# New numbers in the hold-back table of a merged decoder-layer kernel

## The chip, the cores and the metric

One core of one Trainium2 chip runs the whole program. The metric is device time in microseconds of one execution; a kernel's time is the median of its runs. "PE" is the tensor engine, "DVE" the vector engine, "ACT" the scalar engine, "POOL" GpSimd, "SP" the engine that issues most DMAs.

## The reference

One layer of a hybrid decoder runs over a prompt (512 tokens and 16 meta tokens) and over 8 samples of 8 tokens each, with the same float32 weights. Cut to what matters:

```
xn = rmsnorm(x, ln_mix_pre)
q, k, v, gdn_qkv, z, b, a, gate_a, gate_b = split(xn @ w_in)
o_a = diff_attention(q, k, v)                # samples: 16 cached pages of 128 keys each
o_b = gated_delta(silu(conv(gdn_qkv)), b, a) # 4 heads, a recurrence over chunks
o_b = rmsnorm(o_b) * silu(z)
mix = sigmoid(gate_a) * (rmsnorm(o_a) @ w_branch_a) + sigmoid(gate_b) * (o_b @ w_branch_b)
x = x + rmsnorm(mix @ w_out)
up, gate = split(rmsnorm(x) @ w_ffn_in)
x = x + rmsnorm((gelu(conv(gate)) * up) @ w_down)
```

Outputs are the two activations, the new keys and values, and the new states of the delta rule and of both convolutions.

## The kernel before, in words

Each float32 weight tile is split into a high and a low part (`split`, L314 on ACT and L315 on DVE), and a product is three matmuls: high by high, high by low, low by high (`project`, `dense_steps`). A weight tile is 128 columns of a matrix; the tokens are taken in two halves (256 and 336, or 256 and 322 columns). Such dense products write to PSUM tiles `ps_d`. Weight tiles arrive through SP in three `wraw` buffers. Pages of the key and value cache arrive through SP too, 128 of each, in five `page` buffers of two pages.

The program has three stretches. First the input is normalised and transposed and the queries are made. Then comes a merged stretch. Last come the sum of the branches, the output projection and the feed-forward part.

The merged stretch is where this change lies. `Body.merge` takes several generators, called streams. A stream emits a few instructions, then yields a number. `mm` and `transpose` add the price of each PE instruction to a counter `work`: 0.42 ns for each column of a matmul of the split parts, 1.68 ns for one of plain float32, 0.11 us for a transpose. A stream that has yielded `d` may go on when the counter has grown by `d`. So the number is a distance in PE work: while a link of one stream runs through DVE or ACT, PE is given that much work of the other streams. Among the streams that may go on, the one that has spent the smallest part of its share goes first. Where none may go on, a counter `idle` grows in steps of 0.1 and counts as work.

`merge` decides the order in which the instructions are written down. The framework under it then takes that order as priority: it may move an instruction that is ready ahead of one that isn't, when it lays down each engine's list. The lists themselves are fixed before the program runs, and each engine works through its own in order, with semaphores for what comes from the others.

The streams:

- `da_main`: `da_keys` makes keys and values of the four prompt heads (hold 21 after the second half of each), `prompt_attention` works through rows of 128 queries (24 after the scores, 25 after the transposes of the weights, 23 after the head norm), then the meta tokens (22).
- `gdn`: for each head h, `gdn_chain` and, beside it, `gdn_project` of head h + 1 (0 after the last convolution). The chain makes decays (1), transposes and norms (2 to 5), the first inverse by DVE alone (`gdn_base`, 12), the rest of the inverse by products (`gdn_solve`, 13 to 17), and then a recurrence: the tail of samples and meta tokens (6, 7, 8), and four chunks, each of `gS` times `kk` to `grhs` (9), `grhs` to `gv` (10), and `gv` to the next `gS` (11). The head ends with the product `z` (`gdn_gate`) and the transposes of `on`. `gdn_solve_tail` has the holds 18 to 20 in a loop over levels.
- `rest`: `sample_attention` for four pairs of samples, first scores against pages of keys (26), the softmax over 2112 columns (27), then products with pages of values (28), the scaling (29), and after each second pair a head norm (30). Then the 16 gates (`gate`), and `branch_a`, the product of `w_branch_a`, which waits for `self.spare`, set when the last head's solve begins.

In the prediction a step of the recurrence is named as in r, v, S with head and chunk: v00 is the product that gives `gv` of head 0, chunk 0, and S20 the one that gives the next state of head 2.

Of the kernel before, what the change touches and what calls it, by code (L numbers as in the profile page):

```python
# [52 lines left out]
def _lay_out_constants():  # L53
# [76 lines left out]


DELAY = (
    10.08, 5.4, 0.6, 0.6, 6.0, 1.3, 0.9, 0.85, 1.32, 1.0, 1.68, 0.17, 26.0, 0.67, 2.93, 0.77,
    0.09, 0.85, 0.38, 2.28, 0.05, 1.54, 0.74, 1.56, 6.12, 0.84, 1.4, 11.52, 1.4, 1.68, 10.28,
)
KEYS = 2
CUT_S = 832
# [2071 lines left out]
```

## Time and profile before

| | |
|---|---|
| runs of the kernel before | 1165.96, 1167.31, 1167.40 us |
| their median | 1167.31 us |
| span of the profiled execution, first to last instruction | 1165.2 us |
| median of the runs less that span | 2.1 us |
| mean granted clock of the tensor engine | 0.995 |
| PE busy from 60 to 640 us | 563.46 of 580 us |
| DMA share from 60 to 640 us | 0.53 |

The page gives the span of the profiled execution; its time as a run is not listed apart. A page lists the busy time of each engine, the busy share in slices of the span, the DMA queues, the chain of work that ended last, and groups of instructions. In the rows of busy time by stretch each engine's busy microseconds stand in the order PE, PEld (weight loads), DVE, ACT, POOL, then the granted clock, the share of the DMA engines and GB/s. A row of the list of waits reads: who waited, for whom, microseconds in total, how often, the longest. A row of a timeline reads: start, duration, engine, line, operation, tiles, count, and in brackets the idle time before it. Matmuls overlap, so the duration of one is longer than its distance to the next.

### The profile page before, as it was taken

The numbers are of one execution on the slowest core, as the hardware profiler recorded it, in microseconds if no ns is written. First come the engines' busy times: TensorE is split into PE (matmuls) and PEld (weight loads), VectorE is DVE, ScalarE is ACT, GpSimd is POOL, SyncE is SP. The second block draws the span as 40 slices with busy tenths as digits, with TensorE's granted clock in tenths as the row PEclk, the third lists the DMA queues.
The fourth block names the chain that finished last, engine by engine and source line by source line (L and its number), as shares of the span: only waits on it lengthen the run. The fifth ranks groups of instructions, "written<-read, shape, count | busy, mean of one in ns | idle before, by whom it ended". The sixth has DMA issues, their size and how long they took to land.

```text
span 1165.2 us, 23602 instructions
## 1 busy us (share of the span) xinstructions
PE 1122.8 (96%) x8683; PEld 1006.0 (86%) x8683; DVE 717.9 (62%) x1875; ACT 540.1 (46%) x1308; POOL 221.2 (19%) x342
## 2 busy tenths in 40 slices
PE   6999999989999999999999999999999999999997
PEld 5987788777777687689999987899999999999996
DVE  5446667578377368357234675399888988842323
ACT  5234545455355355353333345365556555832331
POOL 2122131030020020010000003234444454200000
PEclk9999999999999999999999999999999999999999
DMA  7374333936847766722222364133333332432322
GB/s 205 80 247 139 108 99 109 300 116 206 298 142 240 259 215 201 245 76 73 73 68 71 99 181 159 68 110 101 92 92 103 90 102 73 143 91 78 100 74 82
DMA packets 184347, 157.56 MB, mean 135 GB/s; under 512 B 12570, under 2 KB 146273, under 8 KB 184231
## 3 DMA queue, kind: packets, MB, share of 16 engines
q1 hardware_dynamic: 179713, 147.53, 41.3%
q0 software_dynamic: 3264, 5.16, 1.5%
q10 hardware_dynamic: 1254, 3.35, 1.0%
q8 instruction: 69, 1.13, 0.4%
q14 instruction: 47, 0.39, 0.1%
HBM read 146.12 MB, written 9.88 MB: 134 GB/s over the span
## 4 chain that ended last, share of the span: by engine, by line
PE 75%; issue 11%; DVE 7%; ACT 2%; POOL 2%; DMA 2%; SPq 0%; DVEq 0%; POOLq 0%; ACTq 0%
PE ps_d L272 29%; PE ps_t L272 18%; PE ps_g L272 15%; PE ps_t L420 7%; PE ps_s L272 6%; PE ps_m L272 1%; DMA page<-in_cache_v 1%; DVE cy L650 1%; DMA page<-in_cache_k 1%; DVE row L970 0%; POOL hss L384 0%; DVE row L971 0%; DVE xc L972 0%; DVE wlo L315 0%; ACT KT L1399 0%
## 5 line engine op out<-in xcount | busy, mean ns | idle before, releaser
L272 PE MATMUL ps_d<-xhi,whi 128*128 128x256 f32 (+2 forms) x704 | 218.4, 311 | 0.0
L272 PE MATMUL ps_d<-xhi,wlo 128*128 128x256 f32 (+2 forms) x704 | 213.9, 304 | 0.8 <-DVE wlo L315 0.8
L315 DVE TENSOR_TENSOR wlo<-wraw,whi 128x512 fp32r<-128x512 f32 x196 | 137.3, 717 | 125.1 <-ACT whi L314 123.9
L272 PE MATMUL ps_d<-xlo,whi 128*128 128x256 f32 (+2 forms) x704 | 213.5, 303 | 0.3 <-DVE xlo L315 0.2
L314 ACT CAST whi<-wraw 128x512 fp32r<-128x512 f32 (+1 forms) x198 | 116.6, 612 | 176.1 <-PE ps_d L272 99.7
L272 PEld LDWEIGHTS ps_d<-xhi,whi 128*128 128x128 f32 x704 | 133.9, 190 | 8.1 <-issue 4.6
L272 PEld LDWEIGHTS ps_d<-xlo,whi 128*128 128x128 f32 x704 | 134.0, 190 | 4.5 <-issue 3.3
L272 PEld LDWEIGHTS ps_d<-xhi,wlo 128*128 128x128 f32 x704 | 134.0, 190 | 1.7 <-DVE wlo L315 1.0
L1399 ACT COPY KT<-ps_t 128x512 f32<-128x512 f32 x106 | 57.5, 596 | 37.6 <-PE ps_t L420 36.2
L420 PE MATMUL ps_t<-consts,page 128*128 128x128 f32 x512 | 68.4, 278 | 1.3 <-DMA page<-in_cache_k 1.0
L420 PEld LDWEIGHTS ps_t<-consts,page 128*128 128x128 f32 x512 | 55.8, 140 | 14.7 <-issue 8.4
L272 PE MATMUL ps_t<-fhit,hw 128*128 128x290 f32 x228 | 68.0, 298 | 0.0
L272 PE MATMUL ps_t<-flot,hw 128*128 128x290 f32 x228 | 67.7, 297 | 0.0
L272 PE MATMUL ps_t<-fhit,lw 128*128 128x290 f32 x228 | 67.6, 297 | 0.0
L314 ACT CAST hw<-sw 128x512 fp32r<-128x512 f32 x76 | 47.2, 623 | 41.2 <-PE ps_g L272 19.9
L315 DVE TENSOR_TENSOR lw<-sw,hw 128x512 fp32r<-128x512 f32 x76 | 59.6, 784 | 6.7 <-ACT hw L314 6.6
L272 PEld LDWEIGHTS ps_t<-flot,hw 128*128 128x128 f32 x228 | 43.3, 190 | 0.0
L272 PEld LDWEIGHTS ps_t<-fhit,lw 128*128 128x128 f32 x228 | 43.1, 189 | 0.0
L272 PEld LDWEIGHTS ps_t<-fhit,hw 128*128 128x128 f32 x228 | 43.0, 189 | 0.0
L272 PE MATMUL ps_s<-KT,qb 128*32 128x256 f32 x512 | 37.1, 385 | 0.4
L1887 DVE SCALAR_TENSOR_TENSOR fy<-fpre,fw,fy 128x592 f32<-128x592 f32 x44 | 36.5, 830 | 1.0 <-ACT fy L1885 0.2
L908 POOL DMA_DIRECT2D out_new_gdn_sample<-st x4 | 3.8, 941 | 170.5 <-ACT gv L892 86.0
(688 smaller groups left out, 3025.8 us busy)
## 6 DMA issues: line engine op xcount, KB each, us to landing
page<-in_cache_k SPq DMA_DIRECT2D x128, 256.0 KB, 4.5
page<-in_cache_v SPq DMA_DIRECT2D x128, 256.0 KB, 4.2
wraw<-in_w_in SPq DMA_DIRECT2D x88, 256.0 KB, 2.9
wraw<-in_w_ffn_in SPq DMA_DIRECT2D x50, 256.0 KB, 3.1
wraw<-in_w_down SPq DMA_DIRECT2D x40, 256.0 KB, 3.2
raw<-in_w_ffn_in SPq DMA_DIRECT2D x38, 256.0 KB, 2.8
wraw<-in_w_out SPq DMA_DIRECT2D x16, 256.0 KB, 2.9
x<-in_x_prompt SPq DMA_DIRECT2D x4, 512.0 KB, 8.9
```

Of the source, the lines that this page charges most:

```text
L272: return self.nc.tensor.matmul(out, lhsT, rhs, **kw).ins
L314: self.nc.scalar.copy(hi, raw)
L315: (eng or self.nc.vector).tensor_tensor(out=lo, in0=raw, in1=hi.bitcast(F32), op=ALU.subtract)
L420: self.nc.tensor.transpose(out, in_, self.ident[:k, :k])
L650: nc.vector.scalar_tensor_tensor(out=y, in0=pre[:, j : j + n], scalar=self.cw[:, ch, 24 + j : 25 + j], in1=y, op0=ALU.mult, op1=ALU.add)
L908: nc.gpsimd.dma_start(o["new_gdn_sample"][0, :, h].rearrange("b k v -> k b v"), state)
L1399: copy(kt[:, :, 128 * j : 128 * j + 128], tp)
L1887: nc.vector.scalar_tensor_tensor(out=y, in0=pre[:, j : j + 592], scalar=fw[:, m, 16 + j : 17 + j], in1=y, op0=ALU.mult, op1=ALU.add)
```

## The change

It replaces numbers in the tuple `DELAY`. The tuple has 31 entries, counted from 0; its first row holds 0 to 15, its second 16 to 30. Nothing else changes: neither the instructions nor their number, nor sizes and buffers.

```
 DELAY = (
-    10.08, 5.4, 0.6, 0.6, 6.0, 1.3, 0.9, 0.85, 1.32, 1.0, 1.68, 0.17, 26.0, 0.67, 2.93, 0.77,
-    0.09, 0.85, 0.38, 2.28, 0.05, 1.54, 0.74, 1.56, 6.12, 0.84, 1.4, 11.52, 1.4, 1.68, 10.28,
+    13.61, 3.59, 0.94, 0.6, 6.0, 1.52, 1.66, 1.43, 1.32, 1.05, 0.93, 0.17, 26.0, 0.69, 0.9, 0.77,
+    0.09, 0.85, 0.38, 2.28, 0.14, 0.6, 0.74, 2.36, 6.91, 0.77, 1.4, 5.18, 1.38, 1.46, 12.26,
 )
```

The largest steps, by ratio, are those of 10 (1.68 to 0.93), 14 (2.93 to 0.9), 21 (1.54 to 0.6) and 27 (11.52 to 5.18), which get smaller, and of 2, 6, 7 and 23, which grow by about a half or more. Entry 20 is changed too (0.05 to 0.14), but its loop is empty here.

## The prediction

> **What bounds the kernel now.** I read the page first, then the busy time by stretch, then who TensorE (PE) waited for in the stretch that the table governs, and last the timelines around the longest of those waits.
>
> ```profile
> span 1165.2 us, 23602 instructions
> PE 1122.8 (96%) x8683; PEld 1006.0 (86%) x8683; DVE 717.9 (62%) x1875; ACT 540.1 (46%) x1308; POOL 221.2 (19%) x342
> ...
> 60.00:500.00 440.00, 424.44 (x3672) 333.94 (x3671) 274.60 (x969) 213.63 (x586) 71.82 (x137) 1.00 0.61 195
> 500.00:640.00 140.00, 139.02 (x1046) 134.70 (x1045) 65.52 (x182) 51.02 (x137) 6.39 (x7) 1.00 0.26 69
> 640.00:700.00 60.00, 58.38 (x392) 54.33 (x393) 40.62 (x74) 23.09 (x42) 0.00 (x0) 1.00 0.47 138
> ```
>
> PE is busy for 96% of the span, no other engine for more than 62%: the kernel is as long as PE's work plus PE's pauses. The table removes and adds no instruction; it only changes the order in which merged streams are written down. So the change is worth what it does to PE's pauses between about 60 us and 660 us. From 60 to 500 PE is idle for 440 − 424.44 = 15.6 us, from 500 to 640 for 1.0 us. Nearly all that can be won lies in the first stretch. These are its waits, and under them the one just behind:
>
> ```profile
> PE ps_t L420 <- DVE kn L792: 3.1, 2, 1.6
> PE ps_t L420 <- DVE on L1344: 2.5, 3, 1.1
> PE ps_g L272 <- DVE grhs L882: 1.8, 4, 0.4
> PE ps_s L272 <- DMA page<-in_cache_v: 1.2, 2, 0.8
> PE ps_t L420 <- DMA page<-in_cache_k: 1.0, 1, 1.0
> PE ps_g L272 <- ACT gv L892: 0.7, 2, 0.4
> PE ps_t L420 <- DVE oS L1344: 0.3, 2, 0.2
> ...
> PE ps_d L272 <- DVE gt L1512: 1.4, 1, 1.4
> ```
>
> The largest, kn (3.1 us), stands behind DELAY[4], which keeps its 6.0. The next, on L1344, stands behind DELAY[23], which changes; grhs and gv stand behind DELAY[9] and [10].
>
> **How much the written order rules.** It does not rule alone: the framework moves instructions that are ready ahead of others. In the plan the split of `oa` comes after all sixteen gates; in the trace it begins at 500.1 us, while the blocks of `z` and the gates' matmuls are still to run. A new number is therefore a preference, not a wait, and most of the new numbers will move nothing that PE feels.
>
> ```profile
> L314 ACT CAST pre<-oa x1: 675/675/675, 500.1 to 500.1; 128x578 fp32r<-128x578 f32 x1
> 635.74 0.28 PE L272 MATMUL ps_d<-kt,whi 128*128 128x256 f32 x1
> 637.14 0.31 PE L272 MATMUL ps_d<-kt,whi 128*128 128x322 f32 x1
> ```
>
> The last two rows give the exchange rate. Twelve 256-column matmuls lie between them: 1.40 us, which the code prices at 12 × 256 × 0.42 ns = 1.29. One unit of the table is about 1.085 us of PE. I also worked the merge rule through with the code's prices for both tables, to see which steps change places.
>
> **Part by part.** *DELAY[23], 1.56 to 2.36 (head norm of the prompt).*
>
> ```profile
> 107.95 0.39 PE L272 MATMUL ps_t<-vt,aT 128*128 128x128 f32 x2
> 110.41 0.17 DVE L383 TENSOR_SCALAR hss<-hss 128x4 f32<-128x4 f32 x1
> 112.27 1.14 DVE L1344 SCALAR_TENSOR_TENSOR on<-on,hss,sub 128x128 f32<-128x128 f32 x4 [1.69 <-POOL hss L384]
> 112.77 0.30 PE L420 MATMUL ps_t<-consts,on 128*128 128x128 f32 x1 [1.09 <-DVE on L1344]
> ```
>
> From the last product (ends 108.34) to the end of the norm (113.41) are 5.1 us, or 4.7 units. Both numbers are under it, the new one by less. It puts 0.8 units, 0.87 us, of other work ahead of the transposes. Of three waits (2.5 us, the longest 1.1) two of about 1.1 shrink to 0.2 and the third goes: −2.0 us. Bounds: 0, if that work isn't ready either, and −2.5.
>
> *DELAY[27], 11.52 to 5.18 (softmax of the sample pairs).*
>
> ```profile
> 460.96 0.43 PE L272 MATMUL ps_s<-kTs,qb 128*32 128x64 f32 x16
> 462.23 2.06 ACT L1479 ACTIVATE S<-S,nm 128x2112 f32<-128x2112 f32 x1 [3.45 <-DVE nm L1477]
> 465.21 0.38 PE L420 MATMUL ps_t<-consts,S 128*64 128x128 f32 x2
> ```
>
> The scores end at 461.39, the exponentials at 464.29: 2.9 us, 2.7 units. 5.18 still covers it, 11.52 was four times too long, yet the transposes of S already start 0.9 us after it, since the framework had moved them up. So the gain is about 0; what changes is that the values' pages stand earlier against the solve of the delta rule. Bounds: −1 us (those 0.9) and, if the pages come too late for it, the page waits of 2.2 us once more.
>
> *DELAY[9], [10] (1.0 to 1.05, 1.68 to 0.93; links of the recurrence).*
>
> ```profile
> 490.08 1.07 PE L272 MATMUL ps_s<-page,pT 128*32 128x256 f32 x16
> 491.08 0.49 PE L272 MATMUL ps_g<-grhs,xy 128*128 128x128 f32 x2
> 491.93 0.49 PE L272 MATMUL ps_g<-gv,kn 128*128 128x128 f32 x2 [0.35 <-ACT gv L892]
> 492.86 0.49 PE L272 MATMUL ps_g<-gS,kk 128*128 128x128 f32 x2
> 493.79 0.49 PE L272 MATMUL ps_g<-grhs,xy 128*128 128x128 f32 x2 [0.45 <-DVE grhs L882]
> ...
> 469.42 17.44 SPq L1378 DMA_DIRECT2D page<-in_cache_v  x22
> 486.96 1.49 SPq L310 DMA_DIRECT2D wraw<-in_w_in  x3
> ```
>
> A link without cover costs 0.35 and 0.45 us. In this head (h = 2) the next weights are issued only at 486.96, behind 22 pages that hold the SP queue for 17.4 us, so there is no dense work to put between. A smaller or larger delay brings none. By the worked order the last pages of pair 3 end one step deeper in the recurrence (at S20 instead of v20), so one link more lies beside pages: −0.8 us. Bounds: −2.5 (1.8 + 0.7, all of it) and +5.0: heads 0 and 1 have no such waits, and each would have 2.5 if its cover went.
>
> In head 3, DELAY[10] is felt as an order:
>
> ```profile
> 614.90 0.38 PE L272 MATMUL ps_g<-gS,kk 128*128 128x128 f32 x2
> 616.90 0.39 PE L272 MATMUL ps_g<-grhs,xy 128*128 128x128 f32 x2
> 619.97 0.38 PE L272 MATMUL ps_g<-gv,kn 128*128 128x128 f32 x2
> ...
> 633.40 0.67 PE L420 MATMUL ps_t<-consts,on 128*128 128x128 f32 x5
> 637.29 2.77 DVE L315 TENSOR_TENSOR blo<-ob,bhi 128x578 fp32r<-128x578 f32 x4
> ```
>
> Between grhs and gv lie 3.07 us, two groups of twelve gate matmuls, where the copy needs far less than one (the wait without any cover was 0.35). With 0.93 one group stands there in each link. PE loses nothing, the chain gets shorter. Head 3 then ends beside gates 12 and 13, not beside the first branch (the rows at 633.40 and 637.29). The 2.77 us of `blo` on DVE no longer stand ahead of the branch's evacuation (gt L1512), for which PE waited 1.4 us: −1.4 us. Bounds: −1.4 and +1.4, if another DVE block takes that place.
>
> *DELAY[21], 1.54 to 0.6 (keys and values of the prompt).*
>
> ```profile
> 104.53 0.31 PE L272 MATMUL ps_d<-xhi,wlo 128*128 128x336 f32 x1
> 105.25 0.43 ACT L1170 COPY kvt<-ps_d 128x336 f32<-128x336 f32 x1
> ```
>
> From the last product (ends 104.84) to the end of the copy (105.68) 0.84 us pass; 0.6 units are 0.65 us. That is short by 0.2, eight times (four heads, keys and values): between 0 and +1.5 us. I take +0.7, the middle, as some of the eight have ready work beside them.
>
> *DELAY[14], 2.93 to 0.9 (the solve's inner products).*
>
> ```profile
> 465.43 0.98 PE L272 MATMUL ps_g<-dd,lm 128*128 128x32 f32 x8
> 466.44 0.27 ACT L1031 COPY dd<-ps_g 128x128 f32<-128x128 f32 x1 [0.66 <-PE ps_g L272]
> 467.29 0.98 PE L272 MATMUL ps_g<-dd,xy 128*128 128x32 f32 x8
> ```
>
> The product ends at 466.41, its copy at 466.71; 0.9 units are 0.98 us: covered, 0. If that cover goes, a wait like that for gv (0.35) eight times: +2.8.
>
> The other thirteen: [20] is never reached, since the tail's list of levels is empty. [30], 10.28 to 12.26, can win no more than the 0.3 us of oS. [6] and [7] (0.9 to 1.66, 0.85 to 1.43) have no wait in the list, nor have [0], [1], [2], [5], [13], [24], [25], [28], [29]; moving them costs at most another kn, 1.6 us, and I take 0.
>
> **Sum.** −2.0 − 0.8 − 1.4 + 0.7 = −3.5 us, from 1165.2 to 1161.7. The median of the runs, 1167.31, is 2.1 us over the profiled span, so 1163.8.
>
> **Weighing a rule of the skill.** The rows give PE 15.6 us of idle time from 60 to 500. They also show PEld busy for 333.94 of 440 us (76%) there and 134.70 of 140 (96%) from 500 to 640. The Trainium skill, Perfetto Trace Analysis, Identifying the Most-Contended Engine, says that matmul occupancy is a poor measure of PE's headroom and that the load-weights share should be used. By that rule the room is an estimated 440 − 333.94 / 0.96 = 92 us, not 15.6, though this stretch holds other kinds of matmul than the next. The trace does not decide here what part of it order can reach.
>
> **The rivals.**
> *Slower: the recurrence loses its cover.* With [27] halved, pages are used up sooner beside the solve, and the links of heads 0 and 1 come after them, as in head 2 now. For it: the worked order ends pair 1's pages ahead of the first link (S0) where they went on to v00 before. Against: in those heads dense work of the next head was at hand. It decides where the first wraw issue after the pages is later than the first gS product. Price: the gains of [23] and the end stay out, 2 × 2.5 = +5.0 us: 1172.3.
> *No change: the framework undoes it.* It moved the split of `oa` up, it can restore most of the old order: 1167.3.
> *More than the idle time.* Small pauses under the limit of the waits' list close up too, as PEld's 76% suggests. A tenth of the difference between 424.44 and 333.94 would be 9 us: 1158.3.
>
> **How the numbers follow.** About 0.2% (2.3 us) is what a measurement of this kernel can tell. Forecast 0.40, more 0.07, no change 0.23, slower 0.30. The first two are faster: 0.47. The range: below, the sum's good ends, −2.5 − 1 − 2.5 − 1.4 − 0.3 = −7.7, and a part of the third rival: 1159.0; above, the slower rival: 1172.5.
>
> **What would show it.** Right: on L1344 under 0.7 us in PE's waits; gt L1512 gone at the branch's start; head 3's last transposes of `on` before the last gates. Wrong: grhs and gv over 4 us, with waits in heads 0 or 1; a wait for kvt or dd in PE's list; page waits over 3 us. If none of these rows moves by 1 us, the second rival holds.

## The result, and the profile after

The median of four runs is 1153.18 us (1151.31 to 1154.48), against 1166.91 us (1165.96 to 1167.40) for the kernel before on the same chip: a ratio of 0.9883, 95% interval [0.9869, 0.9897]. That is 13.7 us faster. The direction was forecast; the size was not: 3.5 us were forecast, and the range ended at 1159.0.

The page of the kernel after begins so; busy time falls by 7.5 us on PE and hardly anywhere else:

```profile
span 1152.0 us, 23616 instructions
PE 1115.3 (97%) x8683; PEld 1004.1 (87%) x8683; DVE 717.3 (62%) x1875; ACT 539.0 (47%) x1308; POOL 220.5 (19%) x342
```

Busy time by stretch, after (PE, PEld, DVE, ACT, POOL, granted clock, DMA share, GB/s):

```profile
60.00:160.00 100.00, 98.39 (x784) 81.54 (x783) 62.60 (x233) 46.58 (x124) 23.89 (x52) 1.00 0.53 166
60.00:500.00 440.00, 429.85 (x3765) 343.85 (x3764) 282.07 (x995) 219.52 (x606) 70.41 (x138) 1.00 0.62 196
500.00:640.00 140.00, 139.77 (x1060) 136.77 (x1059) 64.15 (x173) 46.52 (x121) 5.60 (x5) 1.00 0.29 74
60.00:640.00 580.00, 569.62 (x4823) 480.62 (x4822) 346.22 (x1167) 266.03 (x725) 76.01 (x143) 1.00 0.54 167
```

The same view of before, for the two stretches that the prediction does not show:

```profile
60.00:160.00 100.00, 98.39 (x743) 78.88 (x744) 60.95 (x226) 46.31 (x122) 24.42 (x48) 0.98 0.51 161
60.00:640.00 580.00, 563.46 (x4716) 468.64 (x4714) 340.13 (x1151) 264.65 (x721) 78.21 (x143) 1.00 0.53 165
```

By 640 us PE has issued 107 matmuls more than before. At 580 / 4716 = 0.123 us each that is an estimated 13.2 us, the whole difference of the spans (1165.2 − 1152.0). So all of the gain lies in the merged stretch. But PE's idle time there fell only from 16.5 to 10.4 us. More than half of the gain is not in PE's idle time. The first 100 us show it plainest: PE is busy 98.39 us in both kernels, yet after does 41 matmuls more in them, and PEld is 2.7 us busier. Part of this is the granted clock: the profiled execution of before has 3.41 us at half rate here, at 81 us (mean 0.98), and after has none. Those cost up to 1.7 us, or some 13 of the 41 matmuls at 98.39 / 743 = 0.13 us each. The rest I read as pauses of fractions of a microsecond between matmuls, which a busy row covers.

Where the gain falls I took from a sum of my own, an estimate: each PE instruction priced by its columns, both traces compared at the same time. After is ahead by 4.1 us at 160 us, by 4.6 at 240, 8.5 at 260, 8.5 at 480, 12.1 at 500 and 13.7 at 640. So there are four places: the prompt's first heads (4.1, with up to 1.7 of it the clock), head 0's `kn` (3.9), head 2's links (3.6), and the end of head 3 (1.6).

The waits of PE, after, from 55 to 640 us:

```profile
PE ps_t L420 <- DVE on L913: 2.0, 2, 1.3
PE ps_t L420 <- DVE on L1344: 1.8, 3, 0.9
PE ps_s L272 <- DMA page<-in_cache_v: 1.6, 2, 1.2
PE ps_t L420 <- DVE kn L792: 1.2, 1, 1.2
```

The waits for grhs, gv and gt L1512, 3.9 us before, are gone from the list. Those for kn fell from 3.1 to 1.2, those for on L1344 only from 2.5 to 1.8. Those for on L913 rose from 0.9 to 2.0.

Head 2's recurrence, after: SP's queue, then PE.

```profile
441.80 35.45 SPq L1378 DMA_DIRECT2D page<-in_cache_v  x32
477.36 1.83 SPq L310 DMA_DIRECT2D wraw<-in_w_in  x3
...
473.21 0.39 PE L272 MATMUL ps_g<-gS,kk 128*128 128x128 f32 x2
473.35 0.39 PE L272 MATMUL ps_d<-xhi,wlo 128*128 128x322 f32 x1
...
474.43 0.49 PE L272 MATMUL ps_g<-grhs,xy 128*128 128x128 f32 x2
474.68 0.39 PE L272 MATMUL ps_d<-xhi,wlo 128*128 128x322 f32 x1
...
475.27 0.49 PE L272 MATMUL ps_g<-gv,kn 128*128 128x128 f32 x2
475.69 1.07 PE L272 MATMUL ps_s<-page,pT 128*32 128x256 f32 x16
```

Between every two products of a chunk now stands a group of the next head's dense product (ps_d) or of pages. Before, the last links stood bare. The pages end at 485.2 instead of beyond 494, and the weights are issued at 477.36 instead of 486.96. But the recurrence itself begins earlier by as much: its first product of gS and kk stands at 473.21 instead of 483.96. Against it the weights come no earlier, and the last pages stand at the same step in both kernels, behind the third chunk's grhs product. What changed is the dense work kept for the links: from the first gS by kk product to the last, PE starts 24 dense matmuls after and none before. They begin with weights issued ahead of the pages, as SP issues none from 420 to 477.36.

Head 3, after:

```profile
569.59 0.38 PE L272 MATMUL ps_g<-grhs,xy 128*128 128x128 f32 x2
571.23 0.39 PE L272 MATMUL ps_g<-gv,kn 128*128 128x128 f32 x2
...
600.11 0.67 PE L420 MATMUL ps_t<-consts,on 128*128 128x128 f32 x5
603.40 2.77 DVE L315 TENSOR_TENSOR blo<-ob,bhi 128x578 fp32r<-128x578 f32 x4
```

From grhs to gv are 1.64 us here, and 1.4 to 2.0 in the other three links (before, 2.8 to 3.1 in the first three and 1.2 in the last). `blo` starts 16 us ahead of the branch (first product 619.85) instead of in it. From the first product of gS and kk to these transposes are 32.2 us (567.95 to 600.11), against 35.7 before (597.75 to 633.40). So the shorter links bring 3.5 us of the 33.3 by which the head ends earlier; it also starts 29.8 us earlier.

### The profile page after: what moved, and what is told of

It is laid out like the page before. It is cut to its first block, busy times and chain, and to the rows that moved or that the text cites. A ratio compares the mean times of both kernels' runs of the same rounds, so it can differ in the third digit from the quotient of the medians.

```text
span 1152.0 us, 23616 instructions
## 1 busy us (share of the span) xinstructions
PE 1115.3 (97%) x8683; PEld 1004.1 (87%) x8683; DVE 717.3 (62%) x1875; ACT 539.0 (47%) x1308; POOL 220.5 (19%) x342
## 4 chain that ended last, share of the span: by engine, by line
PE 73%; issue 13%; DVE 6%; ACT 3%; POOL 3%; DMA 1%; SPq 0%; DVEq 0%; POOLq 0%; ACTq 0%
PE ps_d L272 26%; PE ps_t L272 18%; PE ps_g L272 15%; PE ps_s L272 7%; PE ps_t L420 7%; ACT KT L1399 1%; PE ps_m L272 1%; DVE cy L650 1%; DMA lk<-in_da_lambda_k 1%; POOL grr L384 1%; POOL gf L384 0%; DVE wlo L315 0%; DMA page<-in_cache_v 0%; POOL hss L384 0%; DVE row L970 0%
## 5 line engine op out<-in xcount | busy, mean ns | idle before, releaser
L272 PE MATMUL ps_s<-page,pT 128*32 128x256 f32 x512 | 35.3, 385 | 1.8 <-DMA page<-in_cache_v 1.6
L272 PE MATMUL ps_s<-KT,qb 128*32 128x256 f32 x512 | 35.7, 385 | 0.6
```

The lines of the kernel that those rows point to most:

```text
L272: return self.nc.tensor.matmul(out, lhsT, rhs, **kw).ins
```

## The experiments

All times are medians of runs beside the kernel before on the same chip, of which the median was 1166.7 to 1167.5 in each group.

**Four parts alone, in the old table.** Two theories: each number acts on its own wait, and the parts add up; or some numbers are right only together.

*Prompt.*

```
-[21] 1.54  [23] 1.56  [24] 6.12  [25] 0.84
+[21] 0.6   [23] 2.36  [24] 6.91  [25] 0.77
```

> The old table with only the four numbers of the prompt's attention new (21, 23, 24, 25). Theory A, every number pays at its own place and the places add up: the changed kernel is about 4 us ahead by 160 us of the span, so about 4 us faster than before (1163). Theory B, the order is one whole, in which any change moves everything behind it, and parts do not add up: anywhere from 4 us faster to 4 us slower, and unrelated to those 4 us.

Measured 1159.72 us, ratio 0.9939 [0.9921, 0.9958]: 7.7 us faster.

*Samples.*

```
-[27] 11.52  [28] 1.4   [29] 1.68  [30] 10.28
+[27] 5.18   [28] 1.38  [29] 1.46  [30] 12.26
```

> The old table with only the four numbers of the sample attention new (27 to 30), above all 27 halved. Theory A: pages stand earlier against the solve, so the recurrence of head 2 has weights at hand; the unfilled links there cost 2.5 us of waits, so 2 to 4 us faster (1164). Theory B: anywhere within 4 us on either side.

Measured 1178.94, 1.0097 [1.0076, 1.0118]: 11.5 us slower, with 8.7 us of waits for pages of values.

*Solve and recurrence.*

```
-[6] 0.9   [7] 0.85  [9] 1.0   [10] 1.68  [13] 0.67  [14] 2.93
+[6] 1.66  [7] 1.43  [9] 1.05  [10] 0.93  [13] 0.69  [14] 0.9
```

> The old table with only the six numbers of the solve and the recurrence new (6, 7, 9, 10, 13, 14). Theory A: head 3's chain ends earlier, so the wait of 1.4 us at the branch goes, and no more than 1 us elsewhere: 1 to 3 us faster (1165). Theory B: anywhere within 4 us on either side.

Measured 1173.40, 1.0054 [1.0038, 1.0069]: 5.9 us slower.

*Set-up of the heads.*

```
-[0] 10.08  [1] 5.4   [2] 0.6   [5] 1.3
+[0] 13.61  [1] 3.59  [2] 0.94  [5] 1.52
```

> The old table with only the numbers of the chain's set-up new (0, 1, 2, 5; 20 is never reached). Theory A: the waits for kn, 3.1 us before and 1.2 in the changed kernel, shrink: 2 to 4 us faster (1164). Theory B: anywhere within 4 us on either side.

Measured 1171.80, 1.0032 [1.0017, 1.0046]: 4.3 us slower.

(Entry 20, whose loop is empty, was changed along with these four, and put back with them below.)

None of the four came where the first theory had put it, and three moved by clearly more than the 4 us that the second allowed. The four sum to +14.0 us where the whole change gives −13.7. So they do not add: some of these numbers belong together.

**Which belong together.** *Samples with solve, old table.*

```
-[6] 0.9   [7] 0.85  [9] 1.0   [10] 1.68  [13] 0.67  [14] 2.93
+[6] 1.66  [7] 1.43  [9] 1.05  [10] 0.93  [13] 0.69  [14] 0.9
-[27] 11.52  [28] 1.4   [29] 1.68  [30] 10.28
+[27] 5.18   [28] 1.38  [29] 1.46  [30] 12.26
```

> The old table with the sample numbers (27 to 30) and the solve numbers (6, 7, 9, 10, 13, 14) new together; alone they cost 11 and 6 us. Theory P, the two are a pair: the halved softmax hold brings the value pages forward, the short holds of the solve let its products alternate with them; either alone leaves one side bare. Then both together are faster than before by 3 to 7 us (1161 to 1164), and the run of page products without a product between them, and its wait for pages of 8.7 us, is gone. Theory S, the parts add up: 17 us slower (1184). Theory B, no structure: anywhere within 10 us of before.

Measured 1160.11, 0.9941 [0.9924, 0.9957]: −6.6 us, where the two alone cost 11.5 and 5.9. They are a pair. The waits for pages of values, 8.7 us with the samples alone, are 2.3. With the prompt's −7.7 that makes −14.3, close to the change's −13.7.

*The new table with the prompt's four put back.*

```
-[21] 0.6   [23] 2.36  [24] 6.91  [25] 0.77
+[21] 1.54  [23] 1.56  [24] 6.12  [25] 0.84
```

> The new table with the four prompt numbers (21, 23, 24, 25) put back. Theory P, with the prompt numbers worth 7 us on their own stretch: 5 to 8 us slower than the changed kernel (1159 to 1161). Theory S: 1174, as the three other groups alone cost 11, 6 and 4. Theory B: anywhere between.

Measured 1158.10, 0.9921 [0.9906, 0.9936]: some 4.4 us over the change (0.9883). In the new table the prompt's four are worth less than the 7.7 us that they win in the old.

*The new table with the set-up put back.*

```
-[0] 13.61  [1] 3.59  [2] 0.94  [5] 1.52
+[0] 10.08  [1] 5.4   [2] 0.6   [5] 1.3
```

> The new table with the set-up numbers (0, 1, 2, 5, 20) put back. Theory P: they do little on their own, 0 to 3 us slower than the changed kernel (1153 to 1156). Theory S: 4 us faster than it (1149), since alone they cost 4. Theory B: as much as 8 us slower.

Measured 1154.61, 0.9889 [0.9873, 0.9904], as the change itself (0.9883): inside the new table the set-up's numbers neither win nor cost anything that can be measured.

*The new table with the long softmax hold.*

```
-[27] 5.18
+[27] 11.52
```

> The new table with entry 27 alone put back to 11.52. Theory P: the pair is broken, the solve runs ahead of the pages and the links lie bare, 3 to 7 us slower than the changed kernel (1156 to 1160), with waits for grhs and gv back in PE's list. Theory of the prediction (a softmax hold that covers is as good as another): within 1 us of the changed kernel.

Measured 1172.12, 1.0037 [1.0017, 1.0057]: set against the change (1.0037 to 0.9883) some 18 us lost by one number. Both theories missed this: one expected 3 to 7 us with waits for grhs and gv, the other at most 1. No wait for grhs or gv is in the list; those for kn are 4.0 us and for pages of values 4.0. SP's queue and PE show the order that came:

```profile
462.19 1.49 SPq L310 DMA_DIRECT2D wraw<-in_w_in  x3
481.69 16.09 SPq L1378 DMA_DIRECT2D page<-in_cache_v  x22
...
475.35 2.05 PE L272 MATMUL ps_g<-st,zk 128*128 128x128 f32 x16
480.04 0.62 PE L272 MATMUL ps_s<-page,pT 128*32 128x256 f32 x2
```

The whole solve, up to `zk` at 475, has gone by before the first page is used at 480. SP issues nothing for 18 us between, and then the pages run beside the recurrence and into the next head's set-up.

**One number at a time, old table.**

```
-[27] 11.52
+[27] 5.18
```

> The old table with entry 27 alone new (5.18). Theory P: the four sample numbers alone cost 11 us because of this one, so 8 to 12 us slower than before (1175 to 1179), with PE's waits for value pages above 5 us and a stretch at half clock behind them. If 28 to 30 carry it: within 2 us of before.

Measured 1181.72, 1.0140 [1.0116, 1.0163]: 14.8 us slower, somewhat more than expected, with 8.2 us of waits for pages of values. So the harm of the four sample numbers comes from [27].

```
-[14] 2.93  [27] 11.52
+[14] 0.9   [27] 5.18
```

> The old table with entries 27 and 14 new: the halved softmax hold and the hold between the solve's products, 2.93 to 0.9. Theory P in its narrow form, these two are the pair: 4 to 8 us faster than before (1159 to 1163), the solve's products between the page products. In its wide form, all ten numbers of sample and solve are needed: no better than before.

Measured 1165.61, 0.9990 [0.9974, 1.0006]. [14] takes back all of what [27] costs. But the −6.6 us of the pair are not there yet: grhs and gv still have 1.6 us of waits in it, so the solve's other numbers ([6], [7], [9], [10], [13]) or the samples' other three are needed for the links. PE starts no dense matmul between the links of head 2 in this run, and 24 in the run of samples with solve. With the six numbers of the solve alone these waits are gone too, though that run is slower.

```
-[21] 1.54
+[21] 0.6
```

> The old table with entry 21 alone new (1.54 to 0.6). By the prediction it costs 0 to 1.5 us. If the 7 us of the four prompt numbers are its own, since transposes and copies of keys and values come earlier and the rows of the prompt start earlier: 5 to 7 us faster (1160 to 1162).

Measured 1167.22, 1.0001 [0.9989, 1.0013]: nothing that can be measured. No wait for kvt came.

```
-[23] 1.56
+[23] 2.36
```

> The old table with entry 23 alone new (1.56 to 2.36). By the prediction 2.0 us faster, from the waits on L1344 (2.5 us before). If the order behind it matters more than that wait: anywhere within 5 us, while the wait itself changes by less than 1 us.

Measured 1165.17, 0.9980 [0.9965, 0.9995]: 1.7 us, and the wait for on L1344 falls from 2.5 to 1.4. Waits that the number doesn't stand ahead of fall as well: kn from 3.1 to 1.8, grhs from 1.8 to 0.9.

**Is it the softmax's cover, or the place of two streams against each other?** By the merge rule worked through (the working isn't shown here), before and after have pages of values and products of the solve by turns, and with [27] alone nearly all pages come first. The traces agree at pair 3: with [27] alone, 64 products of pages, 16 pages, stand from 477.78 us on without a product of the solve between them; before and after have at most 18 without one. Only the difference of two holds decides: [27] ahead of the pages, and [12] ahead of the solve, which the change doesn't touch. So the harm must go if [12] is moved along, and come without [27] if [12] is moved the other way.

```
-[12] 26.0  [27] 11.52
+[12] 20.0  [27] 5.18
```

> Table of before with entry 27 at 5.18 and entry 12 at 20.0 instead of 26.0. Theory of phase (27 counts only by where the values' pages fall against the solve, and the hold ahead of the solve, 12, moves the solve as far as 27 moved the pages; the worked order of pages against solve of pairs 1 to 3 is then again that of before): the 14.8 us that 27 alone cost go, 1163 to 1170 us, and page waits under 3 us where 27 alone had 8.2. Rival (5.18 is too little for the softmax itself, or too much else moves up with it): 12 doesn't mend it, 1178 to 1184 us. Second rival (20.0 no longer covers the first inverse, whatever the phase): slower than before by over 5 us, with a new wait ahead of the solve.

Measured 1165.87, 0.9990 [0.9974, 1.0006]: the 14.8 us are gone, and the waits for pages of values are 2.5 us instead of 8.2.

```
-[12] 26.0
+[12] 32.34
```

> Table of before with only entry 12 at 32.34 instead of 26.0, the solve held back by as much as the new 27 brings the pages forward. Theory of phase: the same harm without any change to the softmax's hold, 1175 to 1184 us, and page waits over 5 us at the pages of pairs 1 to 3. Rival (the harm of 27 alone is that of the softmax's cover): nothing of it, 1163 to 1170 us, as a longer hold only gives more cover to the first inverse.

Measured 1184.21, 1.0145 [1.0121, 1.0169]: 17.5 us slower, with the softmax's hold untouched. Page waits were 4.8 us, just under the 5 expected. Both runs fall to the theory of place, and the cover of the softmax is out as a cause. PE at pair 3's pages, first with [12] at 20.0 beside the short softmax hold:

```profile
470.40 1.07 PE L272 MATMUL ps_s<-page,pT 128*32 128x256 f32 x16
471.89 1.00 PE L272 MATMUL ps_g<-dd,xy 128*128 128x64 f32 x8
473.48 1.07 PE L272 MATMUL ps_s<-page,pT 128*32 128x256 f32 x16
474.48 0.68 PE L272 MATMUL ps_g<-xy,dbig_low 64*64 64x64 f32 x8
```

and with [12] at 32.34 alone, PE and then the stretch's busy time:

```profile
476.86 1.85 PE L272 MATMUL ps_g<-dd,lm 128*128 128x64 f32 x8 [1.08 <-DVE dd L1010]
478.63 3.64 PE L272 MATMUL ps_s<-page,pT 128*32 128x256 f32 x32
483.24 1.93 PE L272 MATMUL ps_s<-page,pT 128*32 128x256 f32 x16 [0.97 <-DMA page<-in_cache_v]
487.73 1.93 PE L272 MATMUL ps_s<-page,pT 128*32 128x256 f32 x16 [2.56 <-DMA page<-in_cache_v]
...
480.00:500.00 20.00, 14.70 (x100) 8.79 (x93) 3.46 (x12) 3.73 (x10) 0.58 (x1) 0.50 0.41 125
```

SP's queue in the latter:

```profile
465.34 17.49 SPq L1378 DMA_DIRECT2D page<-in_cache_v  x22
```

By turns, each group of pages lies in a link of the solve. In one run, PE uses pages faster than SP's queue brings them (eight pages, 32 products, in 3.64 us even at a clock of 0.50, against 22 in 17.49 us, 0.8 each), waits, and then does the solve bare. The granted clock of that stretch is 0.50; more on that below.

*The counterpart in the new table.*

```
-[14] 0.9
+[14] 2.93
```

> The new table with entry 14 back at 2.93. Theory of phase (14 and 27 are a pair): the worked order puts nearly all of the pages of a pair ahead of the rest of the solve, as with 27 alone, so 1163 to 1172 us, 10 to 19 us over the changed kernel, with page waits over 4 us. Rival (14 mended only what the old numbers of the solve made necessary): within 3 us of the changed kernel, 1150 to 1156 us.

Measured 1173.45, 1.0047 [1.0029, 1.0065], with 9.5 us of page waits: set against the change (1.0047 to 0.9883) some 19 us slower, just past the range expected by the theory of place and far from its rival. So [14] is worth 16 to 19 us beside the new [27], and it was put at nothing in the prediction. How much of this goes through the granted clock is estimated at the end.

**What the prompt's gain is made of.**

```
-[24] 6.12  [25] 0.84
+[24] 6.91  [25] 0.77
```

> Table of before with entries 24 (6.12 to 6.91) and 25 (0.84 to 0.77) new. If these two carry the prompt's gain (7.7 us for the four, of which 21 and 23 alone gave -0.3 and 1.7): 1160 to 1163 us. If the gain lies in the four together: 1165 to 1168 us. If they cost, over 1169 us.

Measured 1166.83, 0.9992 [0.9978, 1.0006]. The runs reach from 1160.59 to 1168.17, and follow the mean clock: 0.996 in the fastest, 0.990 in the four of 1166.9 to 1168.2. In the profiled execution (clock 0.996, span 1158.8) the order's gain is there, while PE's idle time changes by only 0.57 us:

```profile
60.00:160.00 100.00, 98.96 (x775) 81.22 (x774) 62.01 (x230) 46.93 (x124) 24.75 (x52) 0.98 0.52 164
```

32 matmuls more than before in the first 100 us, at the same mean clock of 0.98 and with a half-rate stretch near 81 us too.

```
-[23] 1.56  [24] 6.12  [25] 0.84
+[23] 2.36  [24] 6.91  [25] 0.77
```

> Table of before with 23, 24 and 25 new, 21 left at 1.54. If the prompt's gain is 23 together with 24 and 25: 1158 to 1161 us, as with all four (1159.7). If the parts add: 1.7 + 0.2 off, 1164 to 1166 us, and 21, which alone gave nothing, is needed for the rest.

Measured 1160.43, 0.9947 [0.9929, 0.9965]: −6.6 us. This is the prompt's gain within the intervals (0.9939 with [21]); [21] has no measurable part in it.

**A version built on this.** Longer covers for what still waits, with [12] cut so that the solve stays where it was:

```
-[4] 6.0  [12] 26.0  [23] 2.36
+[4] 7.0  [12] 25.0  [23] 4.0
```

> The new table with 23 at 4.0 (the norm took 4.6 to 6.0 us), 4 at 7.0 (wait for kn 1.2 us left) and 12 at 25.0, so that the solve starts where it did and the worked order of pages against solve stays that of the changed kernel. Theory of phase: no harm, and up to 0.9 of the wait for on and the 1.2 for kn go: 1151 to 1153.5 us. Rival (any longer hold costs as much elsewhere): 1154 to 1158 us.

Measured 1157.90, 0.9923 [0.9908, 0.9938]: 4.7 us slower than the change. The rival holds. The waits aimed at did go, on L1344 from 1.8 to 0.7 and kn from the list, but others came:

```profile
PE ps_s L272 <- DMA page<-in_cache_v: 2.3, 2, 1.5
PE ps_t L420 <- DVE gss L759: 1.7, 1, 1.7
PE ps_d L272 <- ACT tail L631: 1.2, 1, 1.2
PE ps_t L272 <- DVE pT L1453: 1.0, 1, 1.0
```

No kernel run here beats the changed one.

## Why the prediction was wrong, point by point

**What held.** PE's pauses in the merged stretch were the thing to count. [21] was put at +0.7; alone it is +0.3 with an interval of −1.3 to +1.5, and no wait for kvt came. Two terms were met in the number and only in part in the mechanism, so some of that is luck. [23] was put at −2.0 and measured −1.7 alone, but its own wait gave 1.1 of the 2.0, and waits elsewhere went. At the end of head 3 the 1.4 us went as forecast, with one gate group in each link and `blo` out of the branch. But the links shortened the chain by only 3.5 us, and where the chain falls decides: with [27] alone, at the old [10], gt L1512 is out of the list too, and in the new table with [14] put back, at the new [10], 1.1 us of it stand. Of the signs named, the one for on L1344 failed: 1.8 us stayed where under 0.7 were expected. None of the signs against it came.

**The step that failed first: rows taken one at a time.** The term of [27] was "about 0", since 5.18 covers the softmax, and that of [14] 0, since 0.9 covers the copy of dd. Both covers are real, and neither decides. A hold also fixes where its stream stands against the others. The wait for kn shows it in small: the prediction set it aside because [4] keeps its value, and it fell from 3.1 to 1.2 us. [27] alone costs 14.8 us, and [14] beside it wins 16.1 (1181.72 to 1165.61); the two zeros stand for numbers of that size, made of waits for pages and of a lower clock, that nearly cancel. The prediction named the mechanism ("the values' pages stand earlier against the solve") and had the worked order at hand, but worked it only for both whole tables, and never for one number alone. The bound of +2.2 us, "the page waits once more", was too small by a factor of nearly seven.

**The term of [9] and [10] was mis-sized.** Forecast −0.8 of a possible −2.5. All 2.5 us of waits went, and by my sum after wins 3.6 us at head 2's links. The argument was that "there is no dense work to put between", since the weights wait behind the pages on SP. That holds of the new weights only: pages and weights came about 10 us earlier, but so did the recurrence, and the last pages do not end one step deeper in it, as the term had it. Dense work with weights already there was left for the links, 24 matmuls where there had been none. The exact entries that do it were not told apart among the solve's and the samples'.

**Thirteen others at 0.** [24] and [25] have no wait in the list and were left out for it. In the trace of the two alone they win some 3 us before 160 us, by the same sum of mine, and no wait in the list accounts for it. That these are pauses inside rows that read as busy is my reading, not shown matmul by matmul.

**The rivals.** The slower one had the right kind of mechanism (pages that leave the chain without cover) at the wrong place and price: 5.0 us, where the runs with [27] or [12] alone lost 14.8 and 17.5. The third rival, given 0.07, was the nearest, with 1158.3. The load-weights share that it went by rose from 468.64 to 480.62 us in the same 580 us, twice as much as the busy share. By the Trainium skill (Perfetto Trace Analysis, Identifying the Most-Contended Engine) that share is the one to judge room by; the trace agrees in that 12.0 us of PEld came in where idle time fell by 6.2. How much of the estimated 92 us can be reached no run shows.

## What to carry to other kernels

A delay in a merged order is two things: a cover for its own latency, and an offset of its stream against all others. Check the second by working the order out for each number alone and for pairs, and look for a stream that comes in one run where it came by turns. Do not conclude from parts: single numbers moved the time by −1.7 to +17.5 us in the old table and by some 18 and 19 us in the new, and the sum of the four parts has the wrong sign. And where PE is busy for 97%, count matmuls done by a given time; less than half of what was won here came out of PE's idle time.

## What the runs showed of the hardware

The granted clock falls to 0.5 for stretches of 3.41 us or a multiple, and how many there are depends on the order. From 60 to 640 us after has none. Before has one, at 81 us:

```profile
75.00:81.00 6.00, 5.99 (x54) 5.79 (x53) 2.16 (x7) 1.11 (x2) 3.07 (x7) 1.00 1.07 368
81.00:84.50 3.50, 3.50 (x13) 2.17 (x12) 1.23 (x7) 2.49 (x5) 0.51 (x1) 0.51 0.91 293
```

With [12] at 32.34 one of 27.3 us begins at 477, the longest wait in the ten microseconds ahead of it being 1.08 us. With [27] alone one of 20.5 us begins at 482, with [14] put back one of 20.5 us at 477, both inside a wait for pages (3.5 and 3.9 us). With the four sample numbers alone one of 34.1 us begins at 470. PE is busy for 22.0, 16.3, 15.4 and 27.8 us of them. Half of that is an estimate of what the half rate cost at most: 11.0, 8.1, 7.7 and 13.9 us, against waits for pages of 4.8, 8.2, 9.5 and 8.7 in the whole merged stretch. By these bounds the half rate can have cost about as much as the waits for pages did, and more in two of the four. The Trainium skill (TensorE: Matmul & The Clock Gate, Part 1: The HAM clock gate) states half rate as the default and an activity window of about 3.4 us. The trace agrees on the rate and on the unit of 3.41 us. At 81 us it does not show the idle window that the page names there as the condition: 5.99 of 6.00 us were busy ahead of the stretch.

The same shows from run to run. Within one kernel the time follows the mean clock by about 1 us for 0.001: a straight line through the 96 runs of before that stand beside the experiments gives 0.9. The estimates that follow take 1 us and bring both sides to a clock of 0.995. [24] and [25] alone then win 4.1 us where the median says 0, [23] 3.5 and the three together 6.9, so that these nearly add. [27] alone costs 4.6 instead of 14.8, [12] at 32.34 costs 5.9 instead of 17.5, and the four sample numbers 0.0 instead of 11.5. In the new table, [14] put back costs 6.9 instead of 20.3. By this estimate most of what a burst of pages costs comes through the clock. Of the change's own 13.7 us about 1.5 are the clock, 0.9965 in the median after against 0.995 in those 96 runs. What in an order brings the half rate about is left open: no run here separates narrow matmuls from short pauses.
